# A fourth unit of seven products in the down chunk pairs of two FFN parts, and last moves on GpSimd's queue

## The chip, the core and the metric

The kernel runs on one core of a Trainium2 chip. The metric is the device time of one execution in microseconds; lower is better. The core has a matrix engine (TensorE, PE in the profile; its weight loads are PEld), a vector engine (VectorE, DVE), a scalar engine (ScalarE, ACT), GpSimd (POOL) and a queue engine that issues most DMAs (SyncE, SP). TensorE reads operands from the on-chip memory SBUF and accumulates in PSUM banks of 128 x 512 floats.

## The reference

One layer of a hybrid encoder over 256 tokens and a model width of 2048, in float32: a mixing part (neighbourhood attention and a recurrent branch), a dense SwiGLU feed-forward part (FFN) with an inner width of 5632, and an embedding that is gated and added to the residual. What the change touches is the FFN and what follows it:

```python
fn = rms_norm(h, g_ffn_pre[i])
ff = (jax.nn.silu(fn @ w_ffn_gate[i]) * (fn @ w_ffn_up[i])) @ w_ffn_down[i]
h = h + rms_norm(ff, g_ffn_post[i])
gate = jax.nn.sigmoid(rms_norm(h, g_ple_pre[i]) @ w_ple_gate[i])
ple = p[i] @ w_ple_proj[i]
h = h + rms_norm(gate * ple, g_ple_post[i])
```

## The kernel before

**Products.** Features lie on the 128 partitions, in blocks of 128; the 256 tokens are two token tiles of 128. A product takes a feature block of one token tile (128 x 128) as the stationary operand and a weight block (128 x 512) as the moving one. For float32 accuracy every operand is split into a high part, rounded to the type that TensorE reads, and a low part, the difference. A product is then three matmuls: high x high, low x high, high x low. They are written by `products` (L684 to L686, twelve matmuls for a tile of two contraction blocks and both token tiles) and by `product` (L695 to L697, one product). A weight tile is 128 x 2 x 512, 512 KB. It is loaded by `load_stream` (L545 in the FFN, L562 elsewhere) on SP's queue into `wr`, `third` or `lower`, cast to its high part on ScalarE by `hi_stream` (L637), and its low part is made on VectorE by `lo_stream` (L650). Both streams go through the list `tiles` in order. The split tiles lie in `wh`, `wl` and, for one of five, `w`.

**Parts and groups.** The FFN is done in three parts of 4, 4 and 3 chunks of the inner width (`PARTS`). In a part come first the up groups, one for each inner chunk (a gate chunk and an up chunk of 512 columns), and then two down groups, each a pair of output chunks of 512 columns. A `Group` has two chunks, so four accumulator banks; groups take turns in two sets of four banks (`acc` and `sm`). In the first two parts a down group contracts over 16 feature blocks, eight pairs, numbered by their first block kx = 0, 2 to 14.

**Units of seven products.** A pair of contraction blocks times two chunks and two token tiles is eight products. For the pairs in `SEVEN_KS` (up) and `DOWN_KS` (down) a Winograd form makes it with seven. It needs sums of feature blocks (S1, S2, S4, S7) and sums of weight blocks. In the arrays one block of such a pair is swapped between its two weight matrices, so that a unit's first two tiles Q and R hold the blocks that are added. A unit j goes in three steps that lie at different places in the order:
- `four(j)`: two tiles, four products (12 matmuls). `sum_stream` (L585, L589, L595) makes three additions of 512 columns on VectorE for them. They are issued in the group before their own, into the accumulators of their own group. When a group's last four is done, `made_of_four` combines the four banks (one copy on ScalarE, four operations on VectorE and another copy), and the group's event `made` is set; everything else of the group waits for it.
- `two(j)`: the tile R, after `sum_stream`, two products (6 matmuls).
- `one(js)`: one product for each unit of `js` (3 matmuls each); two units share a tile. Its weight block is a sum made by `sum_stream`, to which `last_sum` adds one more block of the weights by a DMA with addition on GpSimd's queue (`added`, L606), issued once the four's tile is split.

The remaining pairs are done as usual (`pair`, 24 matmuls each). `issue` writes the order of a group: `FOURS` says ahead of which remaining pair of this group the fours of the next one go, and `TAKEN` how many twos and ones, in a fixed order, go after which pair. The weight sums live in `ple` (eight blocks of 512 columns): two places for the first sum (`T0`, `T1`) and one for each j for the sum that the one waits for (`t0` to `t2`). R lies in one of five `lower` places.

**Feature sums.** For the down groups, `mid_sums` makes them from the turned chunk `mT` with four subtractions on VectorE (L1769) and a split, for the pairs in `DOWN_KS` of that inner chunk; they lie in `sums` (kx 0 and 2) and `s` (kx 4).

**Turning.** A result has tokens on its partitions and must have features there. `moved` turns 32 x 32 squares on VectorE and then moves the squares with 16 DMAs of 32 KB (L348) into `mT`. `pool` says which of the 16 (by i, four with each i) go on GpSimd's queue; the others go on SP's, in line with the weight loads. After the FFN, the new residual `h` is turned for the last projection: three quarters with transposes on TensorE (`transpose_h`, L329), the last quarter with moves (`turn_h`). Two chunks of the embedding (`embedding(2)` and `embedding(3)`) stand between the FFN and the last projection.

**What sets the order.** A planner inside the program (`Plan`) runs while the program is written: each job is a generator that yields an engine and a cost, and the planner issues what it thinks can start first. `plan.main` advances the planned time of TensorE, `plan.run` lets the jobs issue what fits ahead of that time. The outcome is a fixed order on each engine and each queue; on the chip, an instruction at the head of its queue waits for its semaphores and holds what is behind it.

Of the kernel before, what the change touches and what calls it, by code (L numbers as in the profile page):

```python
# [40 lines left out]
DOWN_KS = (0, 2, 4)  # L41
# [197 lines left out]
def layer(ctx: ExitStack, tc: tile.TileContext, a: dict, out: bass.AP):  # L239
# [5 lines left out]
    plan = Plan(wr=R_BUFS, w=W_BUFS, sm=SM_BUFS, acc=4, ev=1, mid=2, bt=2, m2=1, mt=1, sq=1, T0=1, T1=1, T4=1, **{f"{s}{j}": n for s, m, n in (("p", 5, 1), ("t", 3, 0)) for j in range(m)}, wr0=1, w0=1)  # L245
# [109 lines left out]
    def by_tile(v):  # L355
        return v.rearrange("p k (t q) -> p k t q", t=NT)
# [78 lines left out]
    class Group:  # L435
# [23 lines left out]
        def two(self, j):  # L459
            i = len(tiles)  # L460
            tiles.append(None)
            self.twos.append(i)
            lower[self.own[j] + 1] = -1
            segs.append((two_products, self, j, i))

        def one(self, js):
            i = len(tiles)
            tiles.append(None)
            for j in js:
                _, w, n0 = self.chunks[1]  # L470
                late = a[w][n0 // N, self.sevens[j][0] // 2]
                fours[self.own[j]] = (late, i, j, js, self.lhs.ev_sums, self.twos[j])
            segs.append((one_product, self, js, i))

        own, twos, ahead = None, None, 0
# [7 lines left out]
        def issue(self, nxt):  # L483
            if self.own is None:
                self.own = []
            self.twos = []
            if nxt:
                nxt.own = []
            n, m = len(self.rest), len(self.rest) - self.apart
            more = []  # L490
            for js in (range(0, 2), range(2, len(self.sevens))):
                more += [lambda j=j: self.two(j) for j in js if self.sevens]
            for js in (range(0, 2), range(2, len(self.sevens))):
                more += [lambda js=js: self.one(js)] if js and self.sevens else []
            taken = list(TAKEN.get((len(self.sevens), n, self.lhs is hF), ()))

            def take():
                for _ in range(taken.pop(0) if taken else 0):
                    more.pop(0)()

            take()
            for i, k in enumerate(self.rest[:m]):
                for j, at in enumerate(FOURS[n, len(nxt.sevens), (self.lhs is hF) + 2 * (nxt.lhs is hF)] if nxt and nxt.sevens else ()):
# [67 lines left out]
    def sum_stream():  # L571

        for i in sorted(fours):
# [3 lines left out]
            n, b = first_slot[i], (3, 6, 7)[j]  # L577
# [3 lines left out]
            if n:  # L581
                yield ev_half_spilled
# [27 lines left out]
    def last_sum(i):  # L610
        late, last, j, js, _, _ = fours[i]
        b = (3, 6, 7)[j]
# [158 lines left out]
    def one_product(group, js, i):  # L771
        (C1, _, _), _ = group.chunks
        plan.main(0, ev_lo[i, 2], group.made)
        for j in js:
            kx = group.sevens[j][1]
            product(C1.accs[1], block(group.lhs, kx + 1, 1), i, j - js[0], seeded=True)
        spent(i)
# [24 lines left out]
    def more_sums():  # L802
# [7 lines left out]
        for j in range(3):  # L810
            plan.free[f"t{j}"].append(plan.now)
# [768 lines left out]
    def turn_h(c, hi, lo, nxt, gname):  # L1580
# [7 lines left out]
        mT = yield from moved(e, there, "mt", mT_tile, turn=False)  # L1588
# [171 lines left out]
    def mid_sums(mid, kk0, mT):  # L1760
# [9 lines left out]
        if kk0 == 0:  # L1770
            if "sums" not in t2:
                t2["sums"] = t2["pool"].tile([P, 2, 4, S], F32R, tag="h1", name="sums")
            hi, lo = (by_tile(t2["sums"][:, i, :, :]) for i in range(2))
        else:
            hi, lo = (
                by_tile(t2["s"][:, 2 + i, :].rearrange("p (k s) -> p k s", s=S)) for i in range(2)
            )
        yield from split(hi, lo, mT[:, 0:m], m * S, give="mt")
        for i, kx in enumerate(kxs):
            mid.sums[kx] = {  # L1780
                n: tuple(x[:, 2 * i + k, t, :] for x in (hi, lo))
                for n, k, t in (("S2", 0, 0), ("S7", 0, 1), ("S4", 1, 0), ("S1", 1, 1))
# [78 lines left out]
    for part, (f0, f1) in enumerate(PARTS):  # L1861
# [11 lines left out]
        for c in range(0, 4, 2):  # L1873
# [10 lines left out]
                mid, ks, () if end else DOWN_KS[: 2 if last_part else 3], apart=2 if end else 0,  # L1884
# [315 lines left out]
```

## Time and profile before

| | |
|---|---|
| median of 3 runs | 1150.88 us (1150.77 to 1153.72) |
| profiled execution | 1153.04 us, span 1151.0 us |
| TensorE granted clock, mean | 0.999 |
| HBM read and written | 248.07 MB and 9.44 MB |
| one weight tile | 512.0 KB, 4.5 to 6.4 us to landing |

The profile is of one execution; its span runs from the first to the last instruction. Rows of the chain, of waits, of groups and of time are quoted below where they are used. In a row of a group stand line, engine, operation, output and input by the program's names, count, busy time, the mean duration in ns, and the idle time of the engine just before with what ended it. In a row of time stand start, duration, engine, line, output and input. In a row of a window stand the busy time of each engine with its count, the granted clock, the busy share of the DMA engines and GB/s.

### The profile page before, as it was taken

What the parts mean: (1) busy time and instruction counts of PE and PEld (TensorE: products, weight loads), DVE (VectorE), ACT (ScalarE), POOL (GpSimd) and SP (SyncE); (2) the same over time, 40 slices, a digit from 0 to 9 for tenths busy, and PEclk for the clock granted to TensorE, in tenths of its full rate; (3) what the DMA queues carried; (4) which work ended last, traced back from release to release, by engine and by line L of the source; (5) the groups of instructions that cost most, each with busy time, mean ns of one, the idle gap of its engine ahead of it and who ended that gap; (6) DMA issues with size and microseconds to landing.
All of it is one profiled execution on the core that took longest, in us unless ns stands there. A gap on an engine that the chain in (4) does not pass through costs nothing.

```text
span 1151.0 us, 15131 instructions
## 1 busy us (share of the span) xinstructions
PE 1140.0 (99%) x5211; PEld 947.9 (82%) x5211; DVE 909.9 (79%) x1143; ACT 714.4 (62%) x948; POOL 135.3 (12%) x216
## 2 busy tenths in 40 slices
PE   9999999999999999999999999999999999999997
PEld 7888888888888888888888888888888888887786
DVE  6578787888458779988787898988888888759574
ACT  6777877875457645656656556565555565556564
POOL 0000000000000033131100123311111303100000
PEclk9999999999999999999999999999999999999999
DMA  9867666546686996876976786887887687965671
GB/s 325 283 191 219 185 185 206 174 148 206 226 285 178 313 296 212 259 199 213 279 253 221 249 237 211 264 254 207 290 291 256 196 264 249 284 237 203 207 246 75
DMA packets 112573, 266.92 MB, mean 232 GB/s; under 512 B 39280, under 2 KB 46192, under 8 KB 111088
## 3 DMA queue, kind: packets, MB, share of 16 engines
q1 hardware_dynamic: 99568, 243.57, 62.8%
q0 software_dynamic: 12496, 22.03, 9.7%
q8 instruction: 41, 0.67, 0.2%
q10 hardware_dynamic: 432, 0.35, 0.1%
q14 instruction: 36, 0.29, 0.1%
HBM read 248.07 MB, written 9.44 MB: 224 GB/s over the span
## 4 chain that ended last, share of the span: by engine, by line
PE 93%; DMA 2%; DVE 2%; ACT 2%; issue 1%; SPq 0%; ACTq 0%; DVEq 0%
PE acc L685 24%; PE acc L686 24%; PE acc L684 24%; PE acc L696 6%; PE acc L695 6%; PE acc L697 6%; PE tr L329 1%; DVE wl L650 1%; ACT wh L637 1%; DMA sq<-ev 0%; DMA mT<-mid 0%; DMA wr<-in_w_ple_gate 0%; PE pg L360 0%; PE pg L361 0%; DMA av<-in_w_rg_i 0%
## 5 line engine op out<-in xcount | busy, mean ns | idle before, releaser
L650 DVE TENSOR_TENSOR wl<-wr,wh 128x1024 fp32r<-128x1024 f32 (+1 forms) x308 | 368.2, 1210 | 106.9 <-ACT wh L637 104.9
L637 ACT CAST wh<-wr 128x1024 fp32r<-128x1024 f32 (+1 forms) x308 | 318.9, 1043 | 198.9 <-PE acc L685 139.2
L685 PE MATMUL acc<-wh,hT_mix_lo 128*128 128x512 f32 x440 | 171.4, 390 | 0.3 <-DVE hT_mix_lo L318 0.3
L684 PE MATMUL acc<-wh,hT_mix_hi 128*128 128x512 f32 x440 | 171.5, 390 | 0.0
L686 PE MATMUL acc<-wl,hT_mix_hi 128*128 128x512 f32 x440 | 171.2, 389 | 0.0
L348 POOL DMA_DIRECT2D mT<-mid x152 | 89.5, 602 | 559.8 <-DMA ple<-in_w_ffn_up 401.2
L686 PE MATMUL acc<-wl,hT_hi 128*128 128x512 f32 x320 | 124.5, 390 | 0.0
L684 PE MATMUL acc<-wh,hT_hi 128*128 128x512 f32 x316 | 124.4, 394 | 0.0
L685 PE MATMUL acc<-wh,hT_lo 128*128 128x512 f32 x316 | 123.1, 390 | 0.0
L637 ACT CAST wh<-ple 128x1024 fp32r<-128x1024 f32 (+1 forms) x61 | 59.8, 982 | 64.5 <-PE acc L685 30.8
L685 PEld LDWEIGHTS acc<-wh,hT_mix_lo 128*128 128x128 f32 x440 | 82.6, 188 | 18.0 <-DVE hT_mix_lo L318 1.0
L686 PEld LDWEIGHTS acc<-wl,hT_mix_hi 128*128 128x128 f32 x440 | 82.6, 188 | 17.1
L684 PEld LDWEIGHTS acc<-wh,hT_mix_hi 128*128 128x128 f32 x440 | 82.6, 188 | 17.0
L650 DVE TENSOR_TENSOR wl<-ple,wh 128x1024 fp32r<-128x1024 f32 (+1 forms) x61 | 69.1, 1133 | 9.3 <-ACT wh L637 8.7
L686 PEld LDWEIGHTS acc<-wl,hT_hi 128*128 128x128 f32 x320 | 60.1, 188 | 12.9
L685 PEld LDWEIGHTS acc<-wh,hT_lo 128*128 128x128 f32 x316 | 59.4, 188 | 11.7
L684 PEld LDWEIGHTS acc<-wh,hT_hi 128*128 128x128 f32 x316 | 59.4, 188 | 11.3
L637 ACT CAST wh<-third 128x1024 fp32r<-128x1024 f32 x32 | 33.6, 1051 | 21.0 <-PE acc L685 18.8
L650 DVE TENSOR_TENSOR wl<-third,wh 128x1024 fp32r<-128x1024 f32 x32 | 39.1, 1221 | 6.8 <-ACT wh L637 6.6
L606 POOL DMA_DIRECT2D ple<-in_w_ffn_up x27 | 24.0, 891 | 163.5 <-DVE wl L650 97.6
L684 PE MATMUL acc<-wh,hT_ffn_hi 128*128 128x512 f32 x104 | 40.9, 393 | 1.5 <-ACT hT_ffn_hi L316 1.5
L685 PE MATMUL acc<-wh,hT_ffn_lo 128*128 128x512 f32 x104 | 40.8, 393 | 0.5 <-DVE hT_ffn_lo L318 0.5
(439 smaller groups left out, 2386.9 us busy)
## 6 DMA issues: line engine op xcount, KB each, us to landing
wr<-in_w_in SPq DMA_DIRECT2D x77, 512.0 KB, 4.5
wr<-in_w_ffn_gate SPq DMA_DIRECT2D x74, 512.0 KB, 5.4
wr<-in_w_ffn_down SPq DMA_DIRECT2D x63, 512.0 KB, 5.2
wr<-in_w_ffn_up SPq DMA_DIRECT2D x49, 512.0 KB, 5.2
wr<-in_w_out SPq DMA_DIRECT2D x32, 512.0 KB, 4.4
wr<-in_w_ple_gate SPq DMA_DIRECT2D x32, 512.0 KB, 4.6
lower<-in_w_ffn_up SPq DMA_DIRECT2D x21, 512.0 KB, 6.1
third<-in_w_ffn_gate SPq DMA_DIRECT2D x14, 512.0 KB, 6.4
```

The lines of the kernel that those rows point to most:

```text
L329: nc.tensor.transpose(tr[:, b, t * P : (t + 1) * P], e[:, t, sl], ident)
L348: (nc.gpsimd if i in pool else nc.sync).dma_start(dst[32 * j : 32 * j + 32, :, :, i, :], src[32 * i : 32 * i + 32, :, :, j, :],)
L606: nc.gpsimd.dma_start(dst, src, accum_op=ALU.add)
L637: nc.scalar.copy(his[i][:, 0 : src.shape[1], :] if n == 2 else his[i][:, j, :], src)
L650: nc.vector.tensor_tensor(out=los[i][:, m, :], in0=src, in1=f32(his[i][:, m, :]), op=ALU.subtract)
L684: nc.tensor.matmul(accs[t], hi[:, sl], his[i][:, j, :], start=st, stop=False, **group)
L685: nc.tensor.matmul(accs[t], lo[:, sl], his[i][:, j, :], start=False, stop=False, **group)
L686: nc.tensor.matmul(accs[t], hi[:, sl], los[i][:, j, :], start=False, stop=sp, **group)
L695: nc.tensor.matmul(dst, x[0], wh, start=start, stop=False, skip_group_check=seeded)
L696: nc.tensor.matmul(dst, x[1], wh, start=False, stop=False, skip_group_check=seeded)
L697: nc.tensor.matmul(dst, x[0], wl, start=False, stop=stop, skip_group_check=seeded)
```

## The change

In the first two parts each down group has four units of seven products (kx 0, 2, 4, 6) and four remaining pairs, in place of three and five. `OUT` gives the block of `ple` for each j; j = 3 takes block 1, a new place `t3`. The feature sums of kx 4 and 6 are split in two steps: those of kx 4 go to `s`, those of kx 6 go into columns of the second token tile in the even blocks of the part's own feature tiles, which no unit reads. `TAKEN` and `FOURS` are keyed by kinds of groups (up or down, and the number of units), and steps are written out: digits are twos, `a` is the one of units 0 and 1, `b` the one of the rest. In a down group of four, the ones now come ahead of the twos, behind the first pair. In the last turn (`turn_h` for the last projection), the 12 moves with i = 0, 1, 2 go on GpSimd's queue. `products` tells the planner of the two token tiles one after the other, and in the last two embedding chunks lets it issue other work between them.

```diff
-DOWN_KS = (0, 2, 4)
+DOWN_KS = (0, 2, 4, 6)
+OUT = (3, 6, 7, 1)
...
-("t", 3, 0)
+("t", 4, 0)
...
         def issue(self, nxt):
...
-            more = []
-            for js in (range(0, 2), range(2, len(self.sevens))):
-                more += [lambda j=j: self.two(j) for j in js if self.sevens]
-            for js in (range(0, 2), range(2, len(self.sevens))):
-                more += [lambda js=js: self.one(js)] if js and self.sevens else []
-            taken = list(TAKEN.get((len(self.sevens), n, self.lhs is hF), ()))
+            steps = list(TAKEN[self.kind()]) if self.sevens else []
 
             def take():
-                for _ in range(taken.pop(0) if taken else 0):
-                    more.pop(0)()
+                for x in steps.pop(0) if steps else "":
+                    if x.isdigit():
+                        self.two(int(x))
+                    else:
+                        self.one(range(0, 2) if x == "a" else range(2, len(self.sevens)))
...
-    TAKEN = {(3, 5, True): (0, 2, 3), (3, 5, False): (0, 3, 2), (2, 4, False): (0, 2, 1)}
+    TAKEN = {
+        "up3": ("", "01", "2ab"), "down4": ("", "ab0", "12", "3"), "down2": ("", "01", "a"),
+    }
     FOURS = {
-        (8, 3, 3): (3, 5, 7), (5, 3, 3): (2, 3, 4), (5, 3, 1): (2, 3, 4), (5, 3, 0): (3, 4, 4),
-        (5, 3, 2): (2, 3, 4), (5, 2, 1): (2, 4),
+        ("up0", "up3"): (3, 5, 7), ("up3", "up3"): (2, 3, 4), ("up3", "down4"): (2, 3, 3, 4),
+        ("down4", "down4"): (1, 2, 3, 3), ("down4", "up3"): (1, 2, 3), ("up3", "down2"): (2, 4),
     }
...
     def last_sum(i):
...
-            raws[last] = blocks()[:, 3:7:3, :] if len(js) == 2 else blocks()[:, 7:8, :]
+            raws[last] = blocks()[:, slice(3, 7, 3) if not js[0] else slice(1, 8, 6) if js[1:] else slice(7, 8), :]
...
     def products(...):
...
-                plan.main(6 * MM * len(ts) / NT, ev_lo[p], lhs.ev[kx + j], *after)
-            for t in ts:
+                plan.main(6 * MM / NT, ev_lo[p], lhs.ev[kx + j], *after)
+            for n, t in enumerate(ts):
+                if i and n:
+                    if lhs in pT and i > max(fours):
+                        plan.run()
+                    plan.main(6 * MM / NT)
...
     def turn_h(...):
...
-        mT = yield from moved(e, there, "mt", mT_tile, turn=False)
+        mT = yield from moved(e, there, "mt", mT_tile, turn=False, pool=(0, 1, 2) if nxt is hP else ())
...
     def mid_sums(...):
...
-            hi, lo = (by_tile(t2["sums"][:, i, :, :]) for i in range(2))
+            homes = [by_tile(t2["sums"][:, i, :, :]) for i in range(2)]
+            yield from split(*homes, mT[:, 0:m], m * S, give="mt")
+            homes = [[x[:, 2 * i : 2 * i + 2] for x in homes] for i in range(2)]
         else:
-            hi, lo = (
-                by_tile(t2["s"][:, 2 + i, :].rearrange("p (k s) -> p k s", s=S)) for i in range(2)
-            )
-        yield from split(hi, lo, mT[:, 0:m], m * S, give="mt")
+            homes = [
+                [by_tile(t2["s"][:, 2 + i, :].rearrange("p (k s) -> p k s", s=S)) for i in range(2)],
+                [x[:, 0:8:2, P:S].rearrange("p (k t) q -> p k t q", t=NT) for x in mid.tiles(0)],
+            ]
+            for i, home in enumerate(homes):
+                yield from split(*home, mT[:, 2 * i : 2 * i + 2], 2 * S, give="mt" if i else None)
...
-                mid, ks, () if end else DOWN_KS[: 2 if last_part else 3], apart=2 if end else 0,
+                mid, ks, () if end else DOWN_KS[: 2 if last_part else 4], apart=2 if end else 0,
```

More of the change, by code (lines that the diff above doesn't have):

```diff
@@ L244, in layer @@
     ps = ctx.enter_context(tc.tile_pool(name="ps", bufs=4, space=bass.MemoryType.PSUM))
-    plan = Plan(wr=R_BUFS, w=W_BUFS, sm=SM_BUFS, acc=4, ev=1, mid=2, bt=2, m2=1, mt=1, sq=1, T0=1, T1=1, T4=1, **{f"{s}{j}": n for s, m, n in (("p", 5, 1), ("t", 3, 0)) for j in range(m)}, wr0=1, w0=1)
+    plan = Plan(wr=R_BUFS, w=W_BUFS, sm=SM_BUFS, acc=4, ev=1, mid=2, bt=2, m2=1, mt=1, sq=1, T0=1, T1=1, T4=1, **{f"{s}{j}": n for s, m, n in (("p", 5, 1), ("t", 4, 0)) for j in range(m)}, wr0=1, w0=1)
     def f32(t):
@@ L471, in one, with kind @@
                 late = a[w][n0 // N, self.sevens[j][0] // 2]
-                fours[self.own[j]] = (late, i, j, js, self.lhs.ev_sums, self.twos[j])
+                self.last[j] = (late, i, j, js, self.lhs.ev_sums)
             segs.append((one_product, self, js, i))
-        own, twos, ahead = None, None, 0
+        own, twos, last, ahead = None, None, None, 0
+        def kind(self):
+            return ("up" if self.lhs is hF else "down") + str(len(self.sevens))
         def pair(self, i):
@@ L485, in issue @@
                 self.own = []
-            self.twos = []
+            self.twos, self.last = {}, {}
             if nxt:
@@ L513, in issue @@
                 seg(ch, w, n0, self.lhs, self.rest[m:], first=False)
[L515 removed]
+            for j, x in self.last.items():
+                fours[self.own[j]] = (*x, self.twos[j])
+    TAKEN = {
+        "up3": ("", "01", "2ab"), "down4": ("", "ab0", "12", "3"), "down2": ("", "01", "a"),
+    }
     FOURS = {
[L517 to L518 removed]
+        ("up0", "up3"): (3, 5, 7), ("up3", "up3"): (2, 3, 4), ("up3", "down4"): (2, 3, 3, 4),
+        ("down4", "down4"): (1, 2, 3, 3), ("down4", "up3"): (1, 2, 3), ("up3", "down2"): (2, 4),
     }
@@ L775, in one_product @@
             kx = group.sevens[j][1]
-            product(C1.accs[1], block(group.lhs, kx + 1, 1), i, j - js[0], seeded=True)
+            product(C1.accs[1], block(group.lhs, kx + 1, 1), i, 3 - j if js[0] and js[1:] else j - js[0], seeded=True)
         spent(i)
@@ L809, in more_sums @@
             yield e
-        for j in range(3):
+        for j in range(4):
             plan.free[f"t{j}"].append(plan.now)
```

14 lines of the change are left out of this document (7 added, 7 removed).

## The prediction

> **What bounds the kernel now.** I read the page first: busy shares, chain of waits, costliest groups.
>
> ```profile
> PE 1140.0 (99%) x5211; PEld 947.9 (82%) x5211; DVE 909.9 (79%) x1143; ACT 714.4 (62%) x948; POOL 135.3 (12%) x216
> PE 93%; DMA 2%; DVE 2%; ACT 2%; issue 1%; SPq 0%; ACTq 0%; DVEq 0%
> L650 DVE TENSOR_TENSOR wl<-wr,wh 128x1024 fp32r<-128x1024 f32 (+1 forms) x308 | 368.2, 1210 | 106.9 <-ACT wh L637 104.9
> L637 ACT CAST wh<-wr 128x1024 fp32r<-128x1024 f32 (+1 forms) x308 | 318.9, 1043 | 198.9 <-PE acc L685 139.2
> ```
>
> TensorE is busy for 99% of the span and holds 93% of the chain. The weight splits run ahead of it: the subtraction on VectorE (L650) idles for the cast on ScalarE (L637), and the cast idles mostly for TensorE to free a tile. Next, who TensorE itself waited for; the two rows that touch the change:
>
> ```profile
> PE acc L684 <- ACT hT_ffn_hi L316: 1.5, 1, 1.5
> PE acc L685 <- DVE hT_ffn_lo L318: 0.5, 1, 0.5
> ```
>
> Both lie behind the FFN, where the residual is turned for the last projection; within the FFN there is no row. Then the windows, one per chunk pair: the up group ahead of the first down group, the four down groups that the change rewrites, and last the stretch in which the residual is turned.
>
> ```profile
> core 0: us, PE busy (x) PEld busy (x) DVE busy (x) ACT busy (x) POOL busy (x), PEclk, DMA share, GB/s
> 489.40:530.90 41.50, 41.50 (x184) 34.36 (x184) 35.97 (x40) 24.41 (x27) 11.98 (x19) 1.00 0.72 222
> 530.90:572.40 41.50, 41.50 (x185) 34.36 (x183) 34.63 (x38) 23.10 (x26) 8.14 (x12) 1.00 0.79 235
> 572.40:613.90 41.50, 41.50 (x185) 34.38 (x184) 34.50 (x38) 26.25 (x30) 4.15 (x5) 1.00 0.81 270
> 779.80:821.30 41.50, 41.50 (x185) 34.38 (x184) 35.05 (x39) 23.39 (x26) 8.83 (x13) 1.00 0.83 253
> 821.30:862.80 41.50, 41.50 (x185) 34.38 (x184) 35.62 (x40) 22.38 (x24) 5.58 (x7) 1.00 0.85 285
> 1040.00:1090.00 50.00, 48.00 (x220) 38.75 (x219) 35.05 (x58) 31.38 (x59) 0.00 (x0) 1.00 0.65 211
> ```
>
> In the five groups TensorE never stops and the granted clock is 1.00; VectorE is the next engine, 34.95 us of 41.5 on the mean of the four down windows (84%).
>
> **The fourth unit, on TensorE.** A pair of contraction blocks times two chunks and two token tiles is eight products; a unit makes it with seven. A product is three matmuls (L695 to L697). Their spacing, from six steps in a down group:
>
> ```profile
> 571.26 0.39 PE L685 MATMUL acc<-wh,mid0l 128*128 128x512 f32 x1
> ...
> 572.62 0.39 PE L685 MATMUL acc<-w,mid0l 128*128 128x512 f32 x1
> ```
>
> That should be read as 1.36 / 6 = 0.2267 us a matmul (the 0.39 us shown overlap), so a product is 0.68 us. By hand from the loop, a down group is now 5 pairs of 24 matmuls and 3 units of 21, 183 in all, and 183 x 0.2267 = 41.5 us, the window's length. After: 4 x 24 + 4 x 21 = 180, 40.8 us. Four groups save 12 matmuls: **-2.72 us**, all on the path.
>
> **The fourth unit, beside TensorE.** The pair that goes and the unit that comes both split two tiles. The unit adds one more tile (its "two" products), half a tile (its "one" product shares a tile with the third unit's), and three additions of 512 columns. What each occupies on VectorE, from start to start:
>
> ```profile
> 840.22 1.22 DVE L650 TENSOR_TENSOR wl<-ple,wh 128x1024 fp32r<-128x1024 f32 x1
> 841.36 1.22 DVE L650 TENSOR_TENSOR w<-wr,w 128x1024 fp32r<-128x1024 f32 x1
> ...
> 873.69 0.69 DVE L650 TENSOR_TENSOR w<-ple,w 128x512 fp32r<-128x512 f32 x1
> 874.29 0.68 DVE L589 TENSOR_TENSOR ple<-ple,lower 128x512 f32<-128x512 f32 x1
> ```
>
> 1.14 us a full tile and 0.60 us for 512 columns: 1.14 + (1.14 - 0.60) + 3 x 0.60 = 3.5 us a group. 34.95 + 3.5 = 38.4 of 40.8 us, 94%. ScalarE gains 1.5 casts of 1.04 us, some 1.6 us on the 23.8 us mean. Neither exceeds TensorE. Once per part the wider feature sums add a 512-column split and widen four subtractions, under 5 x 0.60 = 3 us of VectorE in the stretch of an early up group, where the same slack hides it. In the up group ahead of the first down group, the extra four brings 2 x 1.14 + 3 x 0.60 = 4.1 us to VectorE and 12 matmuls, 2.72 us, to TensorE: 40.1 of 44.2 us. The densest place is two fours in a row: 8.2 us of VectorE against 5.44 us of TensorE, 2.8 us short. What covers that is the lead of the splits. Taking the tiles in order and setting the end of each subtraction against the tile's first matmul, the shortest lead in the four down groups is this one:
>
> ```profile
> 574.16 1.23 DVE L650 TENSOR_TENSOR wl<-lower,wh 128x1024 fp32r<-128x1024 f32 x1 [0.89 <-ACT wh L637]
> ...
> 580.56 0.39 PE L695 MATMUL acc<-wh,mid0h 128*128 128x512 f32 x1
> ```
>
> 575.39 to 580.56, 5.2 us; 2.8 us comes off and some 2.4 us stays. The pair of 5.44 us behind it needs only 2.3 us of VectorE and pays it back. So the value I take is 0; without cover each of four groups would lose up to 2.8 us, 11 us in all, which is the upper bound.
>
> The "one" products move from behind the second pair to behind the first, ahead of the "two" products. From the last four to the second "one" tile there lay two pairs, three twos of 1.36 us, a pair and a "one": 21.8 us; now two pairs and a "one", 12.2 us. That tile waits for a weight block added by DMA on GpSimd's queue (the last row is of all transfers into `ple`):
>
> ```profile
> L606 POOL DMA_DIRECT2D ple<-in_w_ffn_down x14: 850/872/977, 504.1 to 975.7; - x14
> L348 POOL DMA_DIRECT2D mT<-mid x152: 582/582/1007, 402.9 to 991.5; - x152
> mT<-mid SPq DMA_DIRECT2D x56, 32.0 KB, 3.9
> mT<-mid POOLq DMA_DIRECT2D x152, 32.0 KB, 4.5
> ple<-in_w_ffn_down POOLq DMA_DIRECT2D x14, 256.0 KB, 5.8
> DMA to landing us min/median/max: 3.9/5.9/9.2
> ```
>
> From the end of the four's own subtraction (some 5 us ahead of its matmuls, 8 us ahead of their end): 0.87 us of issue, 5.8 us of landing, 1.04 us of cast, 1.14 us of subtraction, 8.9 us, so ready about 1 us behind the last four and 11 us early. With the longest landing, 9.2 us, 8 us are left. I count 0. If the block were late, the subtractions of all later tiles would queue behind it, since both split streams go in tile order. The bytes are one more 256 KB load a group on some 10.8 MB (41.5 us at 260 GB/s): 2.4%, a DMA share of 0.85 becoming 0.88. On GpSimd's queue this is 0.87 us more a group.
>
> The Trainium skill (GPSIMD Engine Reference, section 8 "Key points") says that GpSimd shares its SBUF interfaces with VectorE and contends with VectorE instructions that have two SBUF inputs, which all of these are. This case shows subtractions of 1.22 us throughout, though issues on GpSimd do stretch, 582 to 1007 ns. By the rule at its hardest, VectorE would lose each added issue, 0.87 us a group, and stand at 39.3 of 40.8 us; it leaves the sum alone, and speaks for the slower rival below.
>
> **The last moves.** The sixteen moves of the residual's last quarter stand in SP's queue between weight loads, which wait for their buffers:
>
> ```profile
> 1059.67 1.91 SPq L348 DMA_DIRECT2D mT<-mid  x3
> ...
> 1081.07 0.33 SPq L562 DMA_DIRECT2D wr<-in_w_ple_gate  x1
> 1081.45 0.58 SPq L348 DMA_DIRECT2D mT<-mid  x1
> ...
> 1086.60 0.50 PE L684 MATMUL acc<-wh,hT_ffn_hi 128*128 128x512 f32 x1 [1.48 <-ACT hT_ffn_hi L316]
> 1087.12 0.50 PE L685 MATMUL acc<-wh,hT_ffn_lo 128*128 128x512 f32 x1
> ```
>
> They take 22 us to issue, and the last, behind a load, holds TensorE for 1.48 us, and 0.29 us more before the next matmul (0.52 against 0.23). Twelve go to GpSimd's queue, which has nothing else then (no instruction from 1040 to 1090): 12 x 0.58 = 7.0 us, landed by 1059.7 + 7.0 + 4.5 = 1071.2. At the stretched issue of 1.007 us it would be 1076.3; needed at 1085. The four left on SP go one per three of GpSimd's in the plan, so with the loads of the first 7 us; even behind a load that waits 4 us they land by 1077. **-1.77 us**; bounds 0 and -1.77. Next in line are the weight tiles, whose loads on SP lose twelve moves ahead of them.
>
> **Transposes between the halves of an embedding.** The plan may now place a transposed group between the two token tiles of the last embeddings, 0.68 us finer.
>
> ```profile
> 1048.40 1.47 PE L329 MATMUL tr<-ident,h 128*128 128x128 f32 x12
> 1049.63 0.48 PE L684 MATMUL acc<-wh,hT_ffn_hi 128*128 128x512 f32 x1
> 1050.61 0.50 PE L685 MATMUL acc<-wh,hT_ffn_lo 128*128 128x512 f32 x1 [0.50 <-DVE hT_ffn_lo L318]
> ```
>
> 0.98 us from one matmul to the next, 0.75 us lost, to a VectorE that is full there. At best all of it returns; at worst a group of four transposes stands 0.4 us too early and TensorE waits. I take **-0.3 us**, nearer to nothing, as VectorE sets it.
>
> **Sum.** -2.72 - 1.77 - 0.3 = -4.8 us: the profiled execution's span of 1151.0 would be 1146.2. It took 1153.04, 2.04 us around its span; the median of the runs is 1150.88, 2.16 below it, so some of these stalls may be shorter in a plain run. On the median: **1146.1 us**.
>
> **Rivals.**
> - *The moves change nothing.* The last of SP's four moves still stands behind the late load, or plain runs don't have that stall. For it: SP's order is fixed by the plan, and the runs lie 2.2 us below the profiled one. Against it: 13 us of margin. Then 1146.1 + 1.77 = 1147.9. Beside it stands the Trainium skill (DMA: Bandwidth & Descriptors, section "Issuing engines are not separate DMA queues"): issuing elsewhere saves the sequencer's issue time only. Here it is the queue's order that held the move.
> - *The "one" tiles come late.* Sums that the order now wants 9.6 us sooner hold TensorE by some 1 us a group: 1146.1 + 4 = 1150.1. For it: landings up to 9.2 us. Against it: the 8 us above.
> - *VectorE becomes the bound (slower).* In the down groups VectorE idles 41.5 - 34.95 = 6.5 us. If that idle stays, because it is order (subtraction behind cast, additions behind loads) and not surplus, a group takes 38.4 + 6.5 = 44.9 us, 4.1 over TensorE's 40.8; four groups: 1146.1 + 16.4 = 1162.5. It decides from 2.4 us of kept idle, and exceeds the time before from 3.6 us. For it: 94%, and the ring of five buffers now serves four units. Against it: the idle's releaser is the cast, whose own is TensorE.
>
> **How the numbers follow.** Forecast 0.63, unmoved moves 0.19, late "one" tiles 0.07, VectorE 0.11. A measurement here can't tell less than 0.3%, 3.45 us, from no change: faster means below 1147.4, slower above 1154.3. The forecast lies below 1147.4 but for 0.01; the two middle rivals lie within. Faster 0.62, same 0.27, slower 0.11. The range: all of the 0.75 and 1.77 us gives 1145.7, less 1 us for the spread of the runs, 1144.7; above, it takes in the two middle rivals, 1150.3. Some 0.11 above and 0.05 below are left out.
>
> **What would show it.** Right: 5199 matmuls, no wait of TensorE in the down groups, VectorE at about 94% there, the moves landed before 1077 and no wait on `hT_ffn_hi` from them. Wrong: rows of TensorE waiting for L650 or for a "one" tile; a last move still behind a weight load.

## The result, and the profile after

The changed kernel takes 1153.83 us (median of 13 runs, 1152.71 to 1155.56); the kernel before, run beside it, takes 1152.35 us (13 runs, 1150.56 to 1153.72). The ratio is 1.0017, 95% interval 1.0009 to 1.0025: no faster, and some 2 us slower if anything. The prediction, worked out from a median of 1150.88 us before, was 1146.1 us, 1144.7 to 1150.3. One execution of the run without the embedding edit, below, took 6599.62 us and is left out of its ratio. The profiled execution took 1154.53 us, with a span of 1152.7.

First the page of the changed kernel: busy time, shares of the chain of waits by engine, and the two groups of the weight splits. The new lines move the numbers: L650 has become L656, L637 L643, L684 to L686 L694 to L696, L316 and L318 L317 and L319.

```profile
PE 1139.3 (99%) x5199; PEld 946.3 (82%) x5199; DVE 923.4 (80%) x1161; ACT 722.0 (63%) x954; POOL 145.7 (13%) x232
PE 94%; ACT 2%; DVE 2%; DMA 1%; SPq 0%; issue 0%; ACTq 0%
L656 DVE TENSOR_TENSOR wl<-wr,wh 128x1024 fp32r<-128x1024 f32 (+1 forms) x304 | 363.1, 1208 | 107.9 <-ACT wh L643 106.5
L643 ACT CAST wh<-wr 128x1024 fp32r<-128x1024 f32 (+1 forms) x304 | 314.9, 1043 | 183.8 <-PE acc L695 133.3
```

There are 5199 matmuls, twelve fewer, as counted, and VectorE has 13.5 us more work. Nothing here explains a loss. The view of what TensorE waited for does (line, what it waited for, us in total, times, longest):

```profile
PE acc L696 <- DVE wl L656: 3.5, 1, 3.5
PE acc L694 <- ACT hT_ffn_hi L317: 0.3, 1, 0.3
```

The 1.5 us wait for the moved quarter of the residual is gone, and where 0.5 us were waited behind the transposes, 0.3 us are left. In their place stands one wait of 3.5 us, for a weight subtraction, which had none before. Is it in the FFN, as the rivals would have it? The four down groups, in windows of 40.8 us:

```profile
534.80:575.60 40.80, 40.80 (x182) 33.78 (x181) 37.97 (x42) 24.14 (x28) 9.01 (x13) 1.00 0.79 233
575.60:616.40 40.80, 40.80 (x182) 33.78 (x181) 35.50 (x38) 27.58 (x32) 4.89 (x6) 1.00 0.77 257
782.00:822.80 40.80, 40.80 (x181) 33.78 (x181) 38.33 (x43) 25.22 (x27) 9.68 (x14) 1.00 0.79 239
822.80:863.60 40.80, 40.80 (x181) 33.78 (x181) 37.43 (x42) 23.01 (x23) 5.61 (x7) 1.00 0.87 296
```

No: TensorE never stops there, at a clock of 1.00, with VectorE at 37.3 of 40.8 us on the mean. The wait stands behind the FFN, in the last projection. TensorE by time (start, duration, engine, line, output and input):

```profile
1075.02 0.39 PE L694 MATMUL acc<-wh,hT_ffn_hi 128*128 128x512 f32 x1
1075.25 0.39 PE L695 MATMUL acc<-wh,hT_ffn_lo 128*128 128x512 f32 x1
1079.10 0.77 PE L696 MATMUL acc<-wl,hT_ffn_hi 128*128 128x512 f32 x1 [3.46 <-DVE wl L656]
1079.67 0.63 PE L694 MATMUL acc<-wh,hT_ffn_hi 128*128 128x512 f32 x1
1080.10 0.63 PE L695 MATMUL acc<-wh,hT_ffn_lo 128*128 128x512 f32 x1
...
1083.09 0.39 PE L694 MATMUL acc<-wh,hT_ffn_hi 128*128 128x512 f32 x1
```

From 1075.25 to 1083.09 are eleven steps, 2.49 us at 0.2267; they took 7.84, so 5.35 us are lost. The stop is 3.62 us of it (1079.10 less 1075.25 less one step). The other 1.73 us come behind it: the matmuls start 0.43 us apart, about half speed. The windows show the granted clock (third number from the end):

```profile
1078.50:1079.00 0.50, 0.00 (x0) 0.00 (x0) 0.50 (x2) 0.50 (x2) 0.00 (x0) 1.00 0.00 0
1079.50:1081.50 2.00, 2.00 (x6) 1.52 (x6) 2.00 (x2) 0.17 (x1) 0.00 (x0) 0.50 0.64 188
1082.50:1083.00 0.50, 0.50 (x3) 0.39 (x3) 0.35 (x1) 0.00 (x0) 0.00 (x0) 0.94 0.88 172
```

Now follow the missing `wl` back, first on VectorE, then on ScalarE, then to the moves. VectorE:

```profile
1066.34 0.17 DVE L369 RECIPROCAL rstd_p<-rth_ffn 128x2 f32<-128x2 f32 x1 [0.36 <-ACT rth_ffn L367]
1067.28 1.23 DVE L656 TENSOR_TENSOR wl<-wr,wh 128x1024 fp32r<-128x1024 f32 x1 [0.77 <-ACT wh L643]
1075.68 0.48 DVE L319 SCALAR_TENSOR_TENSOR hT_ffn_lo<-mT,vec,hT_ffn_hi 128x256 fp32r<-128x256 f32 x1 [7.18 <-ACT hT_ffn_hi L317]
1077.02 0.88 DVE L319 SCALAR_TENSOR_TENSOR hT_ffn_lo<-mT,vec,hT_ffn_hi 128x256 fp32r<-128x256 f32 x2 [0.86 <-ACT hT_ffn_hi L317]
1077.83 1.22 DVE L656 TENSOR_TENSOR wl<-wr,wh 128x1024 fp32r<-128x1024 f32 x1
```

ScalarE in the same stretch:

```profile
1068.78 1.05 ACT L643 CAST wh<-wr 128x1024 fp32r<-128x1024 f32 x1 [1.54 <-DMA wr<-in_w_ple_gate]
1075.13 0.51 ACT L317 ACTIVATE hT_ffn_hi<-mT,vec 128x256 fp32r<-128x256 f32 x1 [5.30 <-DMA wr<-in_w_ple_gate]
1075.55 1.03 ACT L643 CAST wh<-wr 128x1024 fp32r<-128x1024 f32 x1
1076.49 0.91 ACT L317 ACTIVATE hT_ffn_hi<-mT,vec 128x256 fp32r<-128x256 f32 x2
```

The tile that TensorE lacks, the tenth of the last projection, was cast by 1069.83. Its subtraction could have run then and been done near 1071, over 4 us before TensorE stopped for it. But on VectorE three `hT_ffn_lo<-mT` stand ahead of it, and VectorE takes its instructions in order: it idles 7.18 us for the first of them, runs the three with a gap between, and starts the subtraction at 1077.83. The first `hT_ffn_lo` waits for `hT_ffn_hi` on ScalarE, and that one for the moves. (The row names a weight load as the releaser of 1075.13. But the instruction's input is `mT`, the last of the sixteen moves lands at 1074.88 in the trace, and in most of the runs below the same instruction is released by `mT<-mid`. Where several semaphores fall close together the name is not sure.) The moves themselves, issued on GpSimd, and the landing of all sixteen:

```profile
L349 POOL DMA_DIRECT2D mT<-mid x12: 582/582/587, 1060.3 to 1068.2; - x12
DMA to landing us min/median/max: 1.9/6.1/9.0
```

In the kernel before, where all sixteen went on SP, six subtractions stood ahead of the first `hT_ffn_lo<-mT`, four in one busy stretch and two in the next:

```profile
1071.49 4.87 DVE L650 TENSOR_TENSOR wl<-wr,wh 128x1024 fp32r<-128x1024 f32 x4 [0.77 <-ACT wh L637]
1079.82 2.48 DVE L650 TENSOR_TENSOR wl<-wr,wh 128x1024 fp32r<-128x1024 f32 x2 [3.45 <-ACT wh L637]
1086.58 0.89 DVE L318 SCALAR_TENSOR_TENSOR hT_ffn_lo<-mT,vec,hT_ffn_hi 128x256 fp32r<-128x256 f32 x2 [4.28 <-ACT hT_ffn_hi L316]
```

The planner takes a move to be done 2.0 us after its issue (`LATENCY` in the kernel), where these took 6.1 us at the median. With twelve moves issued early on GpSimd's queue it therefore placed the splits of the turned quarter early, the first three of them ahead of five of these six subtractions.

### The profile page after: what moved, and what is told of

It reads as the page before. It is cut to its first block, busy times and chain, and to the rows that moved or that the text cites. A ratio compares the mean times of both kernels' runs of the same rounds, so it can differ in the third digit from the quotient of the medians.

```text
span 1152.7 us, 15162 instructions
## 1 busy us (share of the span) xinstructions
PE 1139.3 (99%) x5199; PEld 946.3 (82%) x5199; DVE 923.4 (80%) x1161; ACT 722.0 (63%) x954; POOL 145.7 (13%) x232
## 4 chain that ended last, share of the span: by engine, by line
PE 94%; ACT 2%; DVE 2%; DMA 1%; SPq 0%; issue 0%; ACTq 0%
PE acc L696 24%; PE acc L695 24%; PE acc L694 24%; PE acc L707 6%; PE acc L706 6%; PE acc L705 6%; PE tr L330 1%; ACT wh L643 1%; DVE wl L656 1%; DMA wr<-in_w_ple_gate 1%; DMA sq<-ev 0%; ACT junk L1579 0%; DMA wr<-in_w_in 0%; PE pg L362 0%; PE pg L361 0%
## 5 line engine op out<-in xcount | busy, mean ns | idle before, releaser
L656 DVE TENSOR_TENSOR wl<-wr,wh 128x1024 fp32r<-128x1024 f32 (+1 forms) x304 | 363.1, 1208 | 107.9 <-ACT wh L643 106.5
L643 ACT CAST wh<-wr 128x1024 fp32r<-128x1024 f32 (+1 forms) x304 | 314.9, 1043 | 183.8 <-PE acc L695 133.3
L349 POOL DMA_DIRECT2D mT<-mid x164 | 96.3, 600 | 625.6 <-ACT wh L643 482.3
L695 PE MATMUL acc<-wh,hT_mix_lo 128*128 128x512 f32 x420 | 163.6, 390 | 0.3 <-DVE hT_mix_lo L319 0.3
L694 PE MATMUL acc<-wh,hT_mix_hi 128*128 128x512 f32 x420 | 163.7, 390 | 0.0
L696 PE MATMUL acc<-wl,hT_mix_hi 128*128 128x512 f32 x420 | 163.4, 389 | 0.0
L696 PE MATMUL acc<-wl,hT_hi 128*128 128x512 f32 x320 | 124.5, 390 | 0.0
L694 PE MATMUL acc<-wh,hT_hi 128*128 128x512 f32 x316 | 124.4, 394 | 0.0
L643 ACT CAST wh<-ple 128x1024 fp32r<-128x1024 f32 (+1 forms) x65 | 64.9, 1005 | 75.8 <-DVE ple L595 44.6
L695 PEld LDWEIGHTS acc<-wh,hT_mix_lo 128*128 128x128 f32 x420 | 78.8, 188 | 17.2 <-DVE hT_mix_lo L319 1.0
L696 PEld LDWEIGHTS acc<-wl,hT_mix_hi 128*128 128x128 f32 x420 | 78.8, 188 | 16.4
L694 PEld LDWEIGHTS acc<-wh,hT_mix_hi 128*128 128x128 f32 x420 | 78.8, 188 | 16.3
L656 DVE TENSOR_TENSOR wl<-ple,wh 128x1024 fp32r<-128x1024 f32 (+1 forms) x65 | 75.2, 1160 | 7.6 <-ACT wh L643 7.4
L696 PEld LDWEIGHTS acc<-wl,hT_hi 128*128 128x128 f32 x320 | 60.1, 188 | 12.9
L694 PEld LDWEIGHTS acc<-wh,hT_hi 128*128 128x128 f32 x316 | 59.4, 188 | 11.4
L696 PE MATMUL acc<-wl,hT_ffn_hi 128*128 128x512 f32 x104 | 41.4, 398 | 3.5 <-DVE wl L656 3.5
L694 PE MATMUL acc<-wh,hT_ffn_hi 128*128 128x512 f32 x104 | 41.5, 399 | 0.3 <-ACT hT_ffn_hi L317 0.3
L643 ACT CAST wh<-third 128x1024 fp32r<-128x1024 f32 x30 | 31.5, 1051 | 11.3 <-PE acc L695 5.7
```

Source lines behind the costliest of these rows:

```text
L349: (nc.gpsimd if i in pool else nc.sync).dma_start(dst[32 * j : 32 * j + 32, :, :, i, :], src[32 * i : 32 * i + 32, :, :, j, :],)
L643: nc.scalar.copy(his[i][:, 0 : src.shape[1], :] if n == 2 else his[i][:, j, :], src)
L656: nc.vector.tensor_tensor(out=los[i][:, m, :], in0=src, in1=f32(his[i][:, m, :]), op=ALU.subtract)
L694: nc.tensor.matmul(accs[t], hi[:, sl], his[i][:, j, :], start=st, stop=False, **group)
L695: nc.tensor.matmul(accs[t], lo[:, sl], his[i][:, j, :], start=False, stop=False, **group)
L696: nc.tensor.matmul(accs[t], hi[:, sl], los[i][:, j, :], start=False, stop=sp, **group)
```

## The experiments

The theories in the recorded expectations: **A**, the order: an instruction that waits for the moves holds the weight subtractions behind it on VectorE, and its place decides. **B**, the path: moves on GpSimd's queue land too late, whatever the order. **C**, the units: the added work makes VectorE late. **D** to **H** are rivals to parts of A, told in the expectations. All ratios are to the kernel before, run beside on the same chip, with 95% intervals.

**The fourth units alone.** The kernel after without the two other edits.

```diff
-                    if lhs in pT and i > max(fours):
-                        plan.run()
...
-        mT = yield from moved(e, there, "mt", mT_tile, turn=False, pool=(0, 1, 2) if nxt is hP else ())
+        mT = yield from moved(e, there, "mt", mT_tile, turn=False)
```

> The kernel before with only the fourth unit: moves on SP, no planning between the token tiles of the embeddings. A and B: the twelve matmuls alone, 2.7 us below before, ratio 0.9976, and 0.3 us above the run with the embedding halves. C: at or above before.

Measured: 1149.77 us, 0.9975 (0.9965 to 0.9986), that is -2.9 us, where the sum had -2.72. The units do what they were to do, and C falls.

**The change with its last moves back on SP.**

```diff
-        mT = yield from moved(e, there, "mt", mT_tile, turn=False, pool=(0, 1, 2) if nxt is hP else ())
+        mT = yield from moved(e, there, "mt", mT_tile, turn=False)
```

> The changed kernel with the last turn's sixteen moves back on SP's queue; units and embedding halves stay. Theory A (order: the planner takes the moves on GpSimd's queue to land early, so ScalarE and VectorE have the split of the moved quarter ahead of weight splits that TensorE needs first): the 3.5 us wait for L656 and the dip of the granted clock go, the old wait of 1.5 to 2 us is back; 2.75 + 0.3 = 3.0 us below before, ratio 0.997. Theory B (path: moves on GpSimd's queue land late, whatever the order): the same. Theory C (the four units make VectorE late into the last projection): the wait for L656 stays, ratio 1.001 or above.

Measured: 1151.13 us, 0.9980 (0.9971 to 0.9989). The wait for a subtraction is gone and the old one for the moves is back, so the loss comes in with this one line:

```profile
PE acc L694 <- ACT hT_ffn_hi L317: 2.1, 2, 1.8
```

**The moves alone.** The kernel before with nothing but the line that sends the moves to GpSimd's queue.

```diff
-        mT = yield from moved(e, there, "mt", mT_tile, turn=False)
+        mT = yield from moved(e, there, "mt", mT_tile, turn=False, pool=(0, 1, 2) if nxt is hP else ())
```

> The kernel before with nothing changed but the twelve last moves on GpSimd's queue. A and B: TensorE waits some 3.5 us for L650 after the moved quarter's splits and loses 1.7 us more to the clock, against 2.0 us lost there before: 3.3 us slower, ratio 1.003. C: no such wait, 0 to 2 us faster, ratio 0.998 to 1.000.

Measured: 1151.80 us, 0.9990 (0.9982 to 0.9999). That is a miss for A and B: a small gain, not a loss. The ratio alone is one that C allows; the profile is not, for TensorE does wait for a subtraction of the same tile, though briefly, and the clock stays up:

```profile
1076.72 0.39 PE L685 MATMUL acc<-wh,hT_ffn_lo 128*128 128x512 f32 x1
1077.94 0.50 PE L686 MATMUL acc<-wl,hT_ffn_hi 128*128 128x512 f32 x1 [0.83 <-DVE wl L650]
1078.28 0.40 PE L684 MATMUL acc<-wh,hT_ffn_hi 128*128 128x512 f32 x1
```

It stops for 0.99 us (1077.94 less 1076.72 less one step). With the 2.04 us won back (what the kernel before loses around its wait for the moves: 1084.73 to 1087.45 by its rows of TensorE, less three steps), that makes about -1 us, as measured. The written order differs: here one `hT_ffn_lo<-mT` stands ahead of the tenth subtraction, in the changed kernel three. So A had to be narrowed: not whether the splits of the turned quarter come early, but how many stand ahead of that one subtraction.

**The change, with the planner told that the last moves land later.** Queue, transfers and work stay; only the order on ScalarE and VectorE changes. First by 5 us:

```diff
         plan.free["mid"].append(plan.now)
+        if nxt is hP:
+            there.t += 5.0
         yield there
```

> The changed kernel, all moves as changed, but the planner is told that the last turn's moves land 5 us later, which puts two more casts on ScalarE and three more subtractions on VectorE ahead of the moved quarter. A: no wait of TensorE there, and nothing lost to the clock: 2.75 + 0.3 + 2.0 = 5.1 us below before, ratio 0.9956. B: the moves land as late as they did, a wait of 3 us or more stays, ratio 1.000 or above.

Measured: 1147.91 us, 0.9958 (0.9946 to 0.9971). The moves still land late, `hT_ffn_hi` starts at 1073.97 behind them, but the subtractions no longer stand behind it:

```profile
1071.17 1.23 DVE L656 TENSOR_TENSOR wl<-wr,wh 128x1024 fp32r<-128x1024 f32 x1 [0.67 <-ACT wh L643]
1073.37 1.23 DVE L656 TENSOR_TENSOR wl<-wr,wh 128x1024 fp32r<-128x1024 f32 x1 [0.97 <-ACT wh L643]
1074.51 1.28 DVE L319 SCALAR_TENSOR_TENSOR hT_ffn_lo<-mT,vec,hT_ffn_hi 128x256 fp32r<-128x256 f32 x3
```

B falls. This version beats both kernels.

**Without the embedding edit.** Units and moves, but no `plan.run` between the halves of an embedding; the order on VectorE becomes that of the moves alone.

```diff
-                    if lhs in pT and i > max(fours):
-                        plan.run()
```

> The changed kernel without the transposes between the token tiles of the last embeddings: fourth units and moves on GpSimd's queue. On VectorE the order behind the reciprocal is again that of the run with the moves alone: subtraction, one hT_ffn_lo, subtraction, two hT_ffn_lo. Theory A (the place of the tenth tile's subtraction decides, and the embedding edit only tipped it): units -2.7 us and moves -0.9 us as measured by themselves, so ratio 0.997 (0.996 to 0.998) to the kernel before; TensorE waits about 1 us for the subtraction and the granted clock stays at 1.00. Rival D (units and moves together cost the 3.5 us wait, whatever the embeddings do): ratio 1.001 to 1.002, with the wait of 3.5 us and the stretch at a clock of 0.57.

Measured: 1150.44 us, 0.9985 (0.9975 to 0.9994), between the two expectations and nearer to A's. The profile has A's mechanism, one wait of 1.5 us at a clock of 1.00:

```profile
1073.63 0.39 PE L693 MATMUL acc<-wh,hT_ffn_lo 128*128 128x512 f32 x1
1075.53 0.50 PE L694 MATMUL acc<-wl,hT_ffn_hi 128*128 128x512 f32 x1 [1.51 <-DVE wl L656]
1075.86 0.40 PE L692 MATMUL acc<-wh,hT_ffn_hi 128*128 128x512 f32 x1
```

The embedding edit costs nothing by itself (with the moves on SP the ratio is 0.9980 with it and 0.9975 without); it shifts the planner's times enough to tip the order into the costly one. D falls.

**By 1, 3 and 12 us.** The same line as with 5 us, with 1.0, 3.0 and 12.0.

> The changed kernel, with the planner told that the last moves land 1 us later. VectorE's order becomes two subtractions, one hT_ffn_lo, subtraction, two hT_ffn_lo; on ScalarE three casts stand ahead of the first hT_ffn_hi instead of two. Theory A: the tenth tile's subtraction is out of the way, so the 3.5 us wait and the clock's dip go, and the ratio is 0.996 (0.995 to 0.997). Rival E (what costs is the cast held on ScalarE, so that the stop only moves on to the next tile): a wait of TensorE for the eleventh tile's subtraction of 0.8 to 3 us, ratio 0.997 to 1.000.

> As before, told 3 us later: three subtractions ahead of all four hT_ffn_lo. Theory A: no wait for a subtraction, ratio 0.996 (0.995 to 0.997), the same as with 5 us. Rival E: with four hT_ffn_lo together ahead of the twelfth tile's subtraction (1.6 us), a wait there of 0.5 to 2 us, ratio 0.997 to 0.998.

> As before, told 12 us later: seven subtractions ahead of the four hT_ffn_lo, which is the order that the moves on SP had, with the moves landing early all the same. Theory A: the blocks are split some 5 us ahead of their first matmul, no wait over 0.5 us, ratio 0.996 (0.995 to 0.997). Rival G (splitting them so late makes TensorE wait for hT_ffn_hi or hT_ffn_lo as it does with the moves on SP, 2.1 us): ratio 0.998, so that the gain of 3.2 us measured with 5 us would come from the order and none of it from the queue.

Measured: 0.9965 (0.9953 to 0.9978), 0.9963 (0.9950 to 0.9975) and 0.9968 (0.9956 to 0.9981), 1147.46 to 1147.93 us. In none of the three profiles does TensorE wait for a subtraction. With 12 us VectorE's order is that of the changed kernel with its moves on SP, seven subtractions first, and yet nothing waits: `hT_ffn_hi` runs from 1079.8, and TensorE is not held.

```profile
L317 ACT ACTIVATE hT_ffn_hi<-mT,vec x4: 496/496/507, 1079.8 to 1081.0; 128x256 fp32r<-128x256 f32 x4
```

So the wait with the moves on SP (2.1 us above) was one for transfers and not for the order, and the queue does earn its gain. It is the profiles that speak against G and E here: the ratios that they forecast, 0.998 with 12 us and 0.997 with 1 and 3 us, lie within the intervals.

**By 0.4 us, VectorE apart from ScalarE.** On VectorE one subtraction more stands ahead of the first `hT_ffn_lo`; on ScalarE the first `hT_ffn_hi` stands where the changed kernel has it and holds the third cast as there.

> The changed kernel, with the planner told that the last moves land 0.4 us later. On VectorE the tenth tile's subtraction now stands ahead of the first hT_ffn_lo (two subtractions, two hT_ffn_lo, subtraction). On ScalarE the first hT_ffn_hi stands behind two casts, as in the changed kernel itself, and holds the third cast as it did there. Theory A (the subtraction's place on VectorE decides): the tenth tile is split in time and the 3.5 us wait goes; of the eleventh tile's, at most 0.5 us is left; ratio 0.9965 (0.9955 to 0.9975), clock 1.00. Rival E (the cast held on ScalarE decides): the stop only moves to the eleventh tile and stays 2 to 3.5 us long; ratio 0.999 to 1.002.

Measured: 1148.78 us, 0.9971 (0.9960 to 0.9983), no wait of TensorE for a subtraction. VectorE still idles for the moves, 4.44 us, but behind the subtraction and not ahead of it:

```profile
1069.66 1.23 DVE L656 TENSOR_TENSOR wl<-wr,wh 128x1024 fp32r<-128x1024 f32 x1 [1.15 <-PE acc L696]
1075.33 0.89 DVE L319 SCALAR_TENSOR_TENSOR hT_ffn_lo<-mT,vec,hT_ffn_hi 128x256 fp32r<-128x256 f32 x2 [4.44 <-ACT hT_ffn_hi L317]
1076.67 1.23 DVE L656 TENSOR_TENSOR wl<-wr,wh 128x1024 fp32r<-128x1024 f32 x1 [0.45 <-ACT wh L643]
```

The next subtraction ends at 1077.90. TensorE needs it about one tile of 2.72 us behind the place where the changed kernel stopped, near 1078: just in time. E falls: in the changed kernel it is the place on VectorE that decides.

**The other way, by -1 and -2 us.** Now the splits stand still earlier.

> As before, told 1 us earlier: on VectorE the tenth tile's subtraction stands behind two hT_ffn_lo instead of three, and its cast on ScalarE behind two hT_ffn_hi. Theory A: hT_ffn_hi twice from 1075.1, the cast to 1077.1, the subtraction to 1078.3, so TensorE stops for about 3.1 us, against 3.6 us in the changed kernel and 1.5 us in the run without the embedding edit. The run also tells from which length of stop the clock drops. If 3.1 us are not enough: clock 1.00 behind the stop, and ratio 0.998 to 0.9995. If they are: a stretch near 0.5 for 2 to 3 us as in the changed kernel, ratio 0.9995 to 1.001.

> As before, told 2 us earlier: all four hT_ffn_lo stand ahead of the ninth tile's subtraction. Theory A: TensorE stops one tile earlier, near 1072.5, and until the ninth subtraction ends behind the four, near 1080.3: some 7.8 us, and the clock falls behind it by as much or more than in the changed kernel (1.7 to 3 us lost); 4 to 5 us more than the changed kernel, ratio 1.0055 (1.004 to 1.008). Rival H (the stop ends when the moves have landed, wherever the splits stand): it ends near 1079 as in the changed kernel, and the ratio is 1.002 to 1.0035.

With -1 us: 1151.68 us, 0.9994 (0.9985 to 1.0002), within the expectation for a clock that stays up. But the stop isn't the one expected: the moves had landed by 1074.06, and TensorE waits first for the cast and then for the subtraction, 2.05 us and 0.69 us with a matmul between, so that this run says nothing of a stop of 3.1 us. With -2 us: 1157.56 us, 1.0048 (1.0034 to 1.0062), within A's range and above H's, whose upper end of 1.0035 the interval just reaches.

```profile
1071.14 0.39 PE L695 MATMUL acc<-wh,hT_ffn_lo 128*128 128x512 f32 x1
1078.56 0.79 PE L696 MATMUL acc<-wl,hT_ffn_hi 128*128 128x512 f32 x1 [7.03 <-DVE wl L656]
```

TensorE stops one tile earlier than in the changed kernel, as expected. The stop ends at 1078.56, nearer to H's 1079 than to A's 1080.3, because the moves landed earlier here. But it ends 5.3 us after `hT_ffn_hi` could start (1073.26); in the changed kernel it is 4.0 us (1079.10 less 1075.13), without the embedding edit 2.2 us (1075.53 less 1073.31). So it is not the landing alone that ends it, and H falls. What TensorE loses behind the landing grows with what stands ahead of its subtraction. (With -1 us the tenth tile's cast on ScalarE also stands behind two splits of the moved quarter, and 2.05 of the 2.7 us are a wait for that cast; so this row is not VectorE's order alone.)

| ahead of the tenth subtraction, of four `hT_ffn_lo<-mT` | planner told | stop | half clock behind it | ratio |
|---|---|---|---|---|
| none | +0.4 to +12 us | 0 | no | 0.9958 to 0.9971 |
| one (no embedding edit) | - | 1.7 us | no | 0.9985 |
| two | -1 us | 2.7 us in two, the first for the cast | no | 0.9994 |
| three (the change) | - | 3.6 us | 1.7 us lost | 1.0017 |
| four, and the ninth's too | -2 us | 7.2 us | 1.7 us lost | 1.0048 |

## Why the prediction was wrong

**The fourth unit on TensorE, -2.72 us: right.** From the first matmul with `hT_mix` to the last with `mid2h`, by the grouped rows of those tiles, the kernel before and then the changed one:

```profile
L684 PE MATMUL acc<-wh,hT_mix_hi x440: 388/389/481, 350.4 to 983.8; 128*128 128x512 f32 x147
L686 PE MATMUL acc<-wl,mid2h x80: 389/389/389, 984.9 to 1042.7; 128*128 128x512 f32 x80
```

```profile
L694 PE MATMUL acc<-wh,hT_mix_hi x420: 388/389/481, 351.6 to 982.2; 128*128 128x512 f32 x140
L696 PE MATMUL acc<-wl,mid2h x80: 389/389/389, 983.3 to 1041.1; 128*128 128x512 f32 x80
```

692.3 us have become 689.5, 2.8 us less. The later start, 351.6 against 350.4, is no part of the change: up to there the two programs are the same on every engine.

**The fourth unit beside TensorE, 0: right.** No wait in the down groups. VectorE stands at 37.3 of 40.8 us, 91%, where 38.4 and 94% were predicted: a group added 2.4 us to it, not the 3.5 worked out. The lead of the splits and the "one" tiles' margin held, and the two rivals in the FFN (VectorE as the bound, late "one" tiles) didn't come. The subtractions are as long as before, 1208 ns on the mean against 1210, beside 16 more instructions on GpSimd: the rule of contention from the Trainium skill (GPSIMD Engine Reference, section 8 "Key points") left no mark on them.

**Transposes between the halves, -0.3 us: right as a size, but not by the way told.** From the first matmul of the embeddings to the nineteenth with `hT_ffn`, 13.40 us became 13.12. (With the moves on SP it is 13.38 us without the edit and 13.12 with it, so the gain is the edit's.) But no transpose stands between the halves of these embeddings: in both kernels all 24 come behind their last matmul, in the changed one eight in the first block in place of twelve. That the size came out is luck. That the edit would also move the order of another stretch was not weighed.

**The last moves, -1.77 us: this step failed.** Of its figures for the moves, the issue at 582 ns each held, and so did the bound that all have landed by 1077. The landing itself did not: the twelve on GpSimd's queue were expected by 1071.2, with 4.5 us for each, and in the trace the last of them lands at 1074.71. That is still early for the matmul that needs them near 1085. But "bounds 0 and -1.77" had no loss in it, because only TensorE was asked when it needs the blocks. The first to wait for the moves are ScalarE's and VectorE's splits, and in the new order VectorE came to them 7 us ahead of the landing, with weight subtractions behind them. The prediction named what is next in line, "the weight tiles", but for their loads on SP's queue, not for their splits behind the moved quarter's. Even the row was at hand: the splits wait for the moves in the kernel before as well, 4.28 us on VectorE at 1086.58; there six subtractions stood ahead of them, so none of these was held. The term measured +3.3 us (5.35 lost in place of 2.04). Late landing and order make this loss together: the stop ends 4.0 us after the first split could start, so with a landing by 1071.2 it would have ended near 1075.4, when TensorE wanted the tile (1075.48), and cost about nothing; that is an estimate from these rows, which no run tried. The first rival, by which the moves change nothing, doesn't hold either: where the order leaves the subtraction alone, the wait of 2 us is gone, and the ratios go the same way (0.9980 with the moves on SP, 0.9958 to 0.9971 in the five runs without a stop), with intervals that overlap in part.

Summed as measured: -2.8 - 0.28 + 3.3 = +0.2 us; the spans differ by 1.7, of which 1.2 is the later start. By the interval of the ratio the loss is 1.0 to 2.9 us, more than 0.2. The same holds of the runs with -1 and -2 us: with -1, -2.72 - 0.28 - 2.04 + 2.74 makes -2.3 us, and 0.9994 is -0.7. The five without a stop lie 0.2 to 1.7 us above their sum of -5.0 us, so not all of this can be the stop's. The landing, which sets the length of a stop, varies between the profiles (`hT_ffn_hi` could start between 1073.0 and 1075.1), so a plain run may stop longer than the profiled one. The granted clock speaks for that in the runs with -1 us: three of the eleven executions have a mean of 0.996 and took 1152.7 to 1154.1 us, while the profiled one has 0.998 and took 1151.16. The changed kernel's profile, with its drop behind the stop, has 0.996 too, and no run without a drop has a value that low. No trace of those three was kept, and this remainder of a microsecond or two was not settled. With the order mended by 5 us the ratio is 0.9958, and the forecast, 1146.1 to 1150.88 us, was 0.9958 too; that they meet to the last digit is chance, as the other four runs without a stop gave 0.9963 to 0.9971.

## What to carry to other kernels

Where a transfer is moved, ask not only when its data arrive and when the last consumer needs them, but where the first instruction that waits for them stands on its in-order engine, and what is queued behind it. A planner that takes a transfer to land early puts its consumers early; here that cost 5.35 us, against 2.04 us for the late transfer it was to mend. If the planner's landing time is unsure, err late, as far as the data are not needed yet: here +0.4 to +12 us all gave 0.996 to 0.997, as the last consumer wanted them only near 1085, while -1 and -2 us lost 3 to 10 us against that.

## What was not expected of the hardware

**The clock behind a stop.** After stops of 1 to 2 us TensorE went on at full clock. After 3.6 and 7.2 us it came back at 0.50 for some 3.4 us, at a cost of 1.7 us both times. In the changed kernel the drop falls just at the restart: the clock is 1.00 up to 1079.0 and 0.65 on the mean of the next half microsecond. In the run told 2 us earlier the drop itself falls within the stop, between 1075.0 and 1075.5, some 3.5 us after the last matmul ended at 1071.53; columns as in the windows above:

```profile
1074.50:1075.00 0.50, 0.00 (x0) 0.00 (x0) 0.00 (x0) 0.50 (x2) 0.00 (x0) 1.00 0.00 0
1075.00:1075.50 0.50, 0.00 (x0) 0.00 (x0) 0.35 (x1) 0.50 (x2) 0.00 (x0) 0.50 0.00 0
1081.50:1082.00 0.50, 0.50 (x2) 0.36 (x2) 0.42 (x1) 0.00 (x0) 0.00 (x0) 0.68 0.97 369
```

The Trainium skill (TensorE: Matmul & The Clock Gate, Part 1 "The HAM clock gate") states that after an idle window of about 3.4 us the array falls to half rate and needs about as long a busy window to come back. The traces agree, with 3.5 us to the drop and 3.3 us from the restart at 1078.56 to full clock near 1081.8. So the price of a wait has a step, in these runs somewhere between 2.05 and 3.6 us: the stop of 3.6 us cost 5.35.

**The landing of small moves.** In the stretch after 1055, beside weight loads on SP, the same 32 KB moves took 4.3 us at the median when all sixteen stood on SP (the first row, the kernel before), and 6.1 us when twelve stood on GpSimd's queue (the two rows behind it, the changed kernel):

```profile
mT<-mid SPq DMA_DIRECT2D x16, 32.0 KB, 4.3
mT<-mid POOLq DMA_DIRECT2D x12, 32.0 KB, 6.1
mT<-mid SPq DMA_DIRECT2D x4, 32.0 KB, 7.2
```

The four that stayed on SP took 7.2 us at the median, and the longest landing of all, 9.0 us, is one of theirs. So the moves as a whole land more slowly when the sixteen are issued within 9 us instead of 22; whether the queue or the density does it was not tried.
